# A decoder block with 32 experts on one core: expert weights in 4-MB loads, and four blocks of the next expert ahead of a down product

## The chip, the cores and the metric

The kernel runs on one core of one Trainium2 chip. The metric is device time in microseconds. Three runs of the kernel before took 1317.76, 1319.06 and 1319.45 us; the median is 1319.06.

## The reference

One decoder block over 256 tokens of 1024 features in float32: a hybrid mixer (state space and gated branch), cross-attention into 256 memory tokens, and a layer of 32 experts of which each token uses four. Most of the weights, 32 x 12 MB, belong to the experts:

```python
logits = (xt @ w_router + b_router)
top_v, top_i = lax.top_k(logits, 4)
gates = sum(one_hot(top_i, 32) * softmax(top_v)[..., None], axis=1)
def expert_step(acc, p):
    wgu, bgu, wd, bd, g = p
    hgu = xt @ wgu + bgu                       # 1024 -> 2 x 1024
    gate = minimum(hgu[:, :1024], 7.0)
    up = clip(hgu[:, 1024:], -7.0, 7.0)
    y = ((up + 1.0) * gate * sigmoid(1.702 * gate)) @ wd + bd
    return acc + g[:, None] * y
x = LN(ALPHA * x + acc)
```

## The kernel before, in words

The first stage, until about 392 us, does mixer, attention and router. Its weights come in 1-MB units, which are split in two parts for exact float32 products. It then turns to the experts, and nearly all that the change touches is there.

The experts run one after the other, each with room for 64 tokens (`CAP`); two neighbours make a `Pair`. Per pair, `onehot` builds a selection matrix, four `gather` calls (four products of PE each) collect the tokens' features of the pair, one eviction by ACT and one by DVE behind each, and `weights` prepares the scatter. Per expert, `gate_up` returns two functions. `products(k)` multiplies block k of 128 input features: four products of 512 columns, two each for gate and up, which run side by side in two column halves of PE. There are eight blocks an expert. `swiglu` adds the bias by four bf16 products, and runs the chain gc, sg, uc, gc, uc: minimum on DVE, sigmoid on ACT, clip, product and last product on DVE. `hidden_t` transposes the result uc by four PE transpositions and copies it to hT on ACT. `down` multiplies hT with the 4 MB of down weights, 16 products into y. After the second expert of a pair `scatter` copies y to ys (three ACT copies) and adds the pair's outputs to the tokens by four products and four DVE additions into acc, which lies in the tile cd.

`expert_w` loads the weights. The order of use is one long stream of units of 1 MB, a slot of 8192 bytes a partition. The first 22 units are loaded into slots that the first stage frees (`FIRST`); all later ones go round a ring of 20 slots in units of two, 2 MB, one DMA on SyncE's (SP's) queue with rows of 16384 bytes. A unit is issued when the products that read the slots before are done, and each SP issue waits behind the one before it. The last ten loads are 1 MB again. In the source, two blocks (`AHEAD = 2`) of the next expert stand between an expert's swiglu and its hidden_t. The engines run their instructions in the order of the built program; the framework orders them when it builds it, from the source's order, the dependencies and a cost model of its own, so the source's order is not always the program's.

Three pieces of work stand between the experts: `overflow_table` after expert 14, `add_rest` after expert 16 (the residual and the bias of the down product, with 32-row products; its bias rows come by two SP loads into tiles that scatter uses too), and `last_norm` after expert 20. The last expert's down product is cut in four pieces of 256 columns (`down_piece`, `scatter_piece`), then `finish` normalizes and stores.

Of the kernel before, what the change touches and what calls it, by code (L numbers as in the profile page):

```python
# [49 lines left out]
def block_kernel(ctx: ExitStack, tc: tile.TileContext, a, out):  # L50
# [13 lines left out]
    big = ctx.enter_context(tc.tile_pool(name="big", bufs=1))  # L64

    def two(tag, dt=F32):

        return big.tile([P, 2, 2048], dt, tag=tag, name=uniq(tag))
# [134 lines left out]
    def w_parts():  # L203
        t = two(("t01", "t23")[tcount[0] % 2], F32R).rearrange("p q (i c) -> p q i c", i=2)
        tcount[0] += 1
        return [[t[:, q, i] for q in range(2)] for i in range(2)]
# [123 lines left out]
    mh, ml = feat("ab")  # L330
# [32 lines left out]
    xh, xl = feat("xhl")  # L363
# [21 lines left out]
    gvu = two("ab")  # L385
    gv = gvu[:, 0].rearrange("p (c d) -> p c d", c=2)
# [20 lines left out]
    uT = gvu[:, 1].rearrange("p (k t) -> p k t", k=KB)  # L407
# [192 lines left out]
    ysh, ysl = feat("ab")  # L600
# [81 lines left out]
    mh, ml = feat("ab")  # L682
# [13 lines left out]
    xh, xl = feat("xhl")  # L696
# [294 lines left out]
    ucount = [0]  # L991

    def expert_w(src, apart=False):

        i = ucount[0]
        ucount[0] += 1
        if 2 * i < len(FIRST):
            t = []
            for h in range(2):
                name = FIRST[2 * i + h]  # L1000
                with tc.issue_after(wload[PHASE_A.index(FIRST_AFTER.get(name, ("wo", 3)))].ins):
                    if name in SLOTS:
                        t.append(bt(name))
                    elif name == "d":
                        t.append(cd[:, 1])
                    else:
                        if h == 0:
                            both = two(name)
                        t.append(both[:, h])
                    nc.sync.dma_start(t[h], src[:, h])  # L1010
            return t
        name = RING[(i - len(FIRST) // 2) % len(RING)]
        if name in SLOTS:
            at = SLOTS.index(name)
            t = arena[:, at:at + 2, :]
        else:
            t = two(name)
        if apart:
            for h in range(2):
                nc.sync.dma_start(t[:, h], src[:, h])  # L1020
        else:
            nc.sync.dma_start(t, src)
        return [t[:, h] for h in range(2)]

    def gate_up(src, sel, xe, before=None, last=False):
# [40 lines left out]
    def down(src, odd, hT, y, apart=False, between=None):  # L1066

        for u in range(2):
            if u and between is not None:
                between()  # L1070
            w = expert_w(src(u), apart)
            for b in range(4):
                k = 4 * u + b
                for n in range(2):
                    o = 64 * (n ^ odd)
                    te.matmul(y[n][o:o + 64, :], hT[:, b, 64 * u:64 * u + 64],  # L1076
                              w[b // 2][:, b % 2 * D + n * 512:b % 2 * D + (n + 1) * 512], start=(k == 0), stop=(k == KB - 1))

    def scatter(y, PT, first=False):
        ys = [wk.tile([P, 512], F32, tag="ux", name=uniq("ys")) for n in range(2)]  # L1080
        se.activation(ys[0], y[0], AF.Copy)  # L1081
        se.activation(ys[1][0:64, :], y[1][64:128, :], AF.Copy)
        se.activation(ys[1][64:128, :], y[1][0:64, :], AF.Copy)
        for n in range(2):
            for c in range(2):
                ps = pst("sm", 2)
                te.matmul(ps, PT[:, c, :], ys[n], start=True, stop=True)  # L1087
                av = acc[:, c, n * 512:(n + 1) * 512]
                if first:
                    ve.tensor_copy(av, ps)  # L1090
                else:
                    ve.tensor_tensor(av, ps, av, ALU.add)  # L1092
# [42 lines left out]
    AHEAD = 2  # L1135
# [20 lines left out]

    def begin(e):
        xg = pairs[e // 2].xg
        current[e] = gate_up(lambda u: a["w_gu"][e, u], i96[:, e:e + 1], lambda k: xg[:, k, e % 2 * CAP:(e % 2 + 1) * CAP],
                             lambda k: before(e, k), e == NE - 1)  # L1160
# [4 lines left out]
    for e in range(NE - 2):  # L1165
# [3 lines left out]
        uc = swiglu()  # L1169
# [19 lines left out]
    for k in range(AHEAD, KB):  # L1189
        current[ea][0](k)  # L1190
    uc = current[ea][1]()
    begin(eb)
    for k in range(AHEAD):
        current[eb][0](k)
    hT = hidden_t(uc)
    for k in range(AHEAD, KB):
        current[eb][0](k)
# [3 lines left out]
    down(lambda u: a["w_down"][ea, u], 0, hT, y, True, lambda: hTb.append(hidden_t(uc)))  # L1201
# [3 lines left out]
    PT = pairs[ea // 2].PT  # L1205
    for q in range(4):
        if q % 2 == 0:
            w = expert_w(a["w_last"][q // 2], True)
        down_piece(hTb[0], w[q % 2], q, ys)
        if q:  # L1210
            scatter_piece(ys, PT, q - 1, st)
# [5 lines left out]
    with tc.For_i(0, nx, 1):  # L1217
# [36 lines left out]
        down(lambda u: a["w_down"][bass.ds(ev, 1), u].rearrange("e p h d -> p (e h) d"), 0, hT, y)  # L1254
# [12 lines left out]
        for i in range(2):  # L1267
# [9 lines left out]
FIRST = ["e1", "k", "g", "gb", "xhl", "xhl", "w3", "w4", "e0", "x0", "ab", "ab", "w5", "w0", "w1", "w2", "t01", "t01", "t23",  # L1277
         "t23", "j", "d"]
SLOTS = ["e1", "k", "g", "gb", "w3", "w4", "e0", "x0", "w5", "w0", "w1", "w2", "j", "h"]
FIRST_AFTER = {"e1": ("z", 1), "k": ("wq", 0), "g": ("wq", 1), "gb": ("wo", 0)}  # L1280

RING = FIRST[0:20:2]

# [15 lines left out]
def arrange(inputs):  # L1299
# [31 lines left out]
    r["w_gu"] = wg.reshape(NE, 4, 2, P, 2 * D).transpose(0, 1, 3, 2, 4)  # L1331
    r["w_down"] = wd.reshape(NE, 2, 4, P, D).transpose(0, 1, 3, 2, 4).reshape(NE, 2, P, 2, 2 * D)
    r["w_last"] = wd[NE - 1].reshape(KB, P, 4, 256).transpose(2, 1, 0, 3).reshape(2, 2, P, 2 * D).transpose(0, 2, 1, 3)
# [22 lines left out]
```

## Time and profile before

| | |
|---|---|
| median of the runs | 1319.06 us |
| the profiled execution's own time | 1316.82 us |
| its span | 1315.1 us |
| PE busy | 1250.8 us, 95% |
| DVE busy | 450.3 us, 34% |
| ACT busy | 315.5 us, 24% |
| bytes by DMA | 472.00 MB, mean 359 GB/s |

The span is the time from the first to the last instruction. A busy time is the sum of the stretches in which an engine has an instruction at work; PE's products are pipelined, and a product in float32 appears as two records. The chain that ended last is 75% PE and 18% DMA over the whole span. A wait is told with what ended it.

### The profile page before, as it was taken

The page shows a single profiled execution, that of the slowest core. Times are in us where ns is not written, and L with a number is a line of the kernel's source. Part 1 is how long each engine was busy: PE and PEld are TensorE (multiplying, and loading weights), DVE is VectorE, ACT ScalarE, POOL GpSimd, SP SyncE. Part 2 cuts the span into 40 slices and gives each one's busy share as a digit, 9 for nine tenths or more (in the row PEclk, how much of TensorE's full clock was granted, in tenths as well). Part 3 has the DMA queues.
Part 4 walks back from the last instruction along what each step waited for, and adds up shares of the span by engine and source line. Part 5 has one row for each costly group of instructions (what it writes and reads, how often), then busy time and mean ns, then how long its engine had stood idle before and what let it go on. Part 6 is the DMA issues. An engine that isn't in the chain of part 4 may idle for free.

```text
span 1315.1 us, 15885 instructions
## 1 busy us (share of the span) xinstructions
PE 1250.8 (95%) x6757; PEld 684.9 (52%) x6758; DVE 450.3 (34%) x791; ACT 315.5 (24%) x536; POOL 29.1 (2%) x49
## 2 busy tenths in 40 slices
PE   6999999999999999999999999999999999989895
PEld 6899899989873443343333433333343433323232
DVE  4569766687441212121221112232221212212124
ACT  4746665444531111111111111101110111101000
POOL 2110000001000000000000000000000000000000
PEclk9999999999999999999999999969999999999998
DMA  9655543586788999999999999999999999999993
GB/s 357 239 176 196 192 161 133 184 290 227 275 322 353 425 426 427 427 427 428 429 428 427 428 428 427 412 428 427 427 428 428 427 428 427 428 427 427 428 424 160
DMA packets 43930, 472.00 MB, mean 359 GB/s; under 512 B 5104, under 2 KB 6928, under 8 KB 10064
## 3 DMA queue, kind: packets, MB, share of 16 engines
q1 hardware_dynamic: 39840, 464.41, 85.9%
q10 hardware_dynamic: 4016, 6.55, 1.6%
q8 instruction: 54, 0.88, 0.3%
q14 instruction: 20, 0.16, 0.0%
HBM read 469.49 MB, written 1.05 MB: 358 GB/s over the span
## 4 chain that ended last, share of the span: by engine, by line
PE 75%; DMA 18%; DVE 3%; ACT 2%; issue 1%; POOL 1%; ACTq 0%; DVEq 0%; SPq 0%; POOLq 0%
PE gu L1037 25%; PE y L1076 14%; DMA t<-in_w_gu_dram 6%; PE mm L255 6%; PE mm L239 5%; PE mm L238 5%; PE mm L237 5%; PE sm L971 4%; PE sm L1087 3%; DMA arena<-in_w_down_dram 3%; DMA ab<-in_w_gu_dram 3%; DMA arena<-in_w_gu_dram 3%; DMA t<-in_w_down_dram 2%; PE sm L1062 1%; DVE t L181 1%
## 5 line engine op out<-in xcount | busy, mean ns | idle before, releaser
L1037 PE MATMUL gu<-arena,cd 128*64 128x512 f32 x1240 | 279.8, 594 | 4.8 <-DMA arena<-in_w_gu_dram 4.8
L1037 PEld LDWEIGHTS gu<-arena,cd 128*64 128x64 f32 x1240 | 86.6, 137 | 171.5 <-issue 157.1
L181 DVE TENSOR_TENSOR t<-arena,t 128x1024 fp32r<-128x1024 f32 (+1 forms) x111 | 131.9, 1210 | 49.6 <-ACT t L180 49.6
L1076 PE MATMUL y<-arena,hT 128*64 128x512 f32 x592 | 140.7, 616 | 6.8 <-ACT hT L1063 5.6
L180 ACT ACTIVATE t<-arena 128x1024 fp32r<-128x1024 f32 (+1 forms) x114 | 113.8, 1038 | 59.2 <-PE mm L255 19.1
L1049 DVE TENSOR_SCALAR gc<-gu 128x512 f32<-128x512 f32 x32 | 22.1, 692 | 297.9 <-PE gu L1044 297.9
L237 PE MATMUL mm<-xhl,t 128*128 128x256 f32 x384 | 110.5, 288 | 0.0
L239 PE MATMUL mm<-xhl,t 128*128 128x256 f32 x384 | 108.8, 283 | 1.7 <-DVE t L181 1.7
L238 PE MATMUL mm<-xhl,t 128*128 128x256 f32 x384 | 108.7, 283 | 0.0
L1050 ACT ACTIVATE sg<-gc 128x512 f32<-128x512 f32 x32 | 20.2, 630 | 342.1 <-DVE gc L1049 342.1
L975 DVE TENSOR_SCALAR cd<-sm,par 128x128 f32<-128x128 f32 x64 | 26.2, 410 | 210.7 <-ACT cd L973 210.5
L1092 DVE TENSOR_TENSOR cd<-sm,cd 128x512 f32<-128x512 f32 x56 | 38.7, 692 | 169.3 <-PE sm L1087 169.3
L1076 PEld LDWEIGHTS y<-arena,hT 128*64 128x64 f32 x592 | 42.6, 140 | 85.9 <-issue 74.7
L1037 PE MATMUL gu<-t,cd 128*64 128x512 f32 x384 | 87.1, 595 | 0.1
L973 ACT ACTIVATE cd<-sm,par 128x128 f32<-128x128 f32 x64 | 29.3, 457 | 227.4 <-PE sm L971 226.0
L971 PEld LDWEIGHTS sm<-pair,arena 128*128 128x128 f32 x512 | 62.0, 191 | 31.7 <-issue 27.2
L239 PEld LDWEIGHTS mm<-xhl,t 128*128 128x128 f32 x384 | 73.5, 191 | 1.9 <-DVE t L181 1.9
L971 PE MATMUL sm<-pair,arena 128*128 128x128 f32 x512 | 71.3, 285 | 3.2 <-ACT pair L989 1.8
L238 PEld LDWEIGHTS mm<-xhl,t 128*128 128x128 f32 x384 | 73.6, 192 | 0.2
L237 PEld LDWEIGHTS mm<-xhl,t 128*128 128x128 f32 x384 | 73.5, 191 | 0.2
L1087 PE MATMUL sm<-ys,pair 128*128 128x512 f32 x120 | 59.1, 615 | 10.4 <-ACT ys L1081 10.2
L1037 PEld LDWEIGHTS gu<-t,cd 128*64 128x64 f32 x384 | 26.5, 137 | 50.3 <-issue 48.3
(314 smaller groups left out, 1447.8 us busy)
## 6 DMA issues: line engine op xcount, KB each, us to landing
arena<-in_w_gu_dram SPq DMA_DIRECT2D x71, 2048.0 KB, 31.8
arena<-in_w_down_dram SPq DMA_DIRECT2D x35, 2048.0 KB, 30.0
arena<-in_wa_dram SPq DMA_DIRECT2D x56, 1024.0 KB, 5.1
t<-in_w_gu_dram SPq DMA_DIRECT2D x22, 2048.0 KB, 33.8
ab<-in_w_gu_dram SPq DMA_DIRECT2D x13, 2048.0 KB, 30.1
xhl<-in_w_gu_dram SPq DMA_DIRECT2D x12, 2048.0 KB, 29.5
t<-in_w_down_dram SPq DMA_DIRECT2D x12, 2048.0 KB, 30.9
arena<-in_w_gu_dram SPq DMA_DIRECT2D x13, 1024.0 KB, 7.3
```

The source lines that it names most:

```text
L180: se.activation(h, src, AF.Copy)
L181: sub_op[0] = (eng or ve).tensor_tensor(l, src, h.bitcast(F32), ALU.subtract)
L237: te.matmul(ps[:, b, :], wh, xh[:, k, :], start=(k == 0), stop=False)
L238: te.matmul(ps[:, b, :], wh, xl[:, k, :], start=False, stop=False)
L239: te.matmul(ps[:, b, :], wl, xh[:, k, :], start=False, stop=(k == KB - 1))
L255: last[0] = te.matmul(res[c], x[:, k, c * P:(c + 1) * P], w[k // 2 % 2][:, k % 2, :], start=(k == 0 and i == 0), stop=(k == KB - 1 and i = ...
L971: te.matmul(pg[:, b, :], x2[:, c, k * P:(k + 1) * P], self.t[:, 0, c, :], start=(c == 0), stop=(c == 1))
L973: se.activation(self.xg[:, k, :], pg[:, 0, :], AF.Identity, bias=b2[:, k:k + 1], scale=g2[:, k:k + 1])
L1037: te.matmul(t[64 * j:64 * j + 64, :], xe(k), ws[k][:, n * D + j * 512:n * D + (j + 1) * 512], start=(k == 0), stop=False)
L1076: te.matmul(y[n][o:o + 64, :], hT[:, b, 64 * u:64 * u + 64], w[b // 2][:, b % 2 * D + n * 512:b % 2 * D + (n + 1) * 512], start=(k == 0), ...
L1087: te.matmul(ps, PT[:, c, :], ys[n], start=True, stop=True)
L1092: ve.tensor_tensor(av, ps, av, ALU.add)
```

## The change

The slots of the ring that were pairs of tiles (`t01`, `t23`, `xhl`, `ab`) become two tiles of four slots, `four0` and `four1`; the other slots lie in fours in the arena. From expert 4 on, a ring load is 4 MB, four slots with rows of 32768 bytes, half of an expert's gate and up weights or all its down weights; experts 0 to 3 keep 2 MB, the last expert and the last down products take smaller ones. The packing of the weights in HBM follows. `AHEAD` is 4, with hidden_t after the third block; scatter is returned as a function that is called behind block 4 of the next expert, whose first four blocks come before the down product; its two half copies change places. The bias rows of the down product go by one load into the free slot `j`, and two tiles of the first stage move to the slots `h` and `j`.

```diff
+    def fours(i, dt):
+        if (i, dt) not in four:
+            four[i, dt] = big.tile([P, 4, 2048], dt, tag=f"four{i}", name=uniq(f"four{i}"))
+        return four[i, dt]
...
-        bd = [wk.tile([NE, 512], F32, tag="ux", name=uniq("bd")) for n in range(2)]
-        for n in range(2):
-            nc.sync.dma_start(bd[n], a["b_down"][:, n * 512:(n + 1) * 512])
+        t = bt("j")
+        nc.sync.dma_start(t[:NE, :D], a["b_down"])
+        bd = [t[:NE, n * 512:(n + 1) * 512] for n in range(2)]
...
+    def expert_w(src, n=1):
+        out = []
+        h = src.shape[1]
+        while len(out) < h:
+            i = ucount[0]
+            if i < len(FIRST):
+                m, name = 1, FIRST[i]
...
+            else:
+                m = min(n, h - len(out))
+                at = (rcount[0] + NRING - len(FIRST) % 4) % NRING
+                assert at % m == 0
+                rcount[0] += m
+                t = slots(RING[at // 4] + at % 4, m)
+                after = ExitStack()
+            ucount[0] += m
+            with after:
+                nc.sync.dma_start(t, src[:, len(out):len(out) + m])
+            out += [t[:, q] for q in range(m)]
+        return out
...
-            if k % 2 == 0:
-                ws[k], ws[k + 1] = expert_w(src(k // 2), last and k == KB - 2)
+            if k % 4 == 0:
+                ws.update(enumerate(expert_w(src(k // 4), n_rows[k // 4]), k))
...
-    AHEAD = 2
+    AHEAD = 4
...
+    def rows_of(e):
+        return (2, 2) if e < 4 else (4, 4)
...
+    ready = []
+    def finish_products(e):
         products, swiglu = current.pop(e)
         for k in range(AHEAD, KB):
             products(k)
+            if ready:
+                ready.pop()()
+        return swiglu()
+
+    for e in range(NE - 2):
+        uc = finish_products(e)
         begin(e + 1)
-        for k in range(AHEAD):
+        for k in range(AHEAD - 1):
             current[e + 1][0](k)
         hT = hidden_t(uc)
+        current[e + 1][0](AHEAD - 1)
...
-        down(lambda u: a["w_down"][e, u], b, hT, y)
+        down(a["w_down"][e], b, hT, y, rows_of(e)[0])
         if b:
...
-            scatter(y, pairs.pop(e // 2).PT, e == 1)
+            ready.append(scatter(y, pairs.pop(e // 2).PT, e == 1))
...
-    down(lambda u: a["w_down"][ea, u], 0, hT, y, True, lambda: hTb.append(hidden_t(uc)))
+    down(a["w_down"][ea], 0, hT, y, 2, lambda: hTb.append(hidden_t(uc)))
...
-FIRST = ["e1", "k", "g", "gb", "xhl", "xhl", "w3", "w4", "e0", "x0", "ab", "ab", "w5", "w0", "w1", "w2", "t01", "t01", "t23",
-         "t23", "j", "d"]
...
+FIRST = ["e1", "k", "g", "gb", "w5", "w0", "xh", "xl", "a", "b", "e0", "x0", "w1", "w2", "j", "w3", "w4", "t0", "t1", "t2", "t3", "d"]
+RING = [8, 0, 12, 4, 16]
...
-    r["w_gu"] = wg.reshape(NE, 4, 2, P, 2 * D).transpose(0, 1, 3, 2, 4)
+    r["w_gu"] = wg.reshape(NE, 2, 4, P, 2 * D).transpose(0, 1, 3, 2, 4)
```

The built program moves instructions in more places than the diff. In the rows below a name before the arrow is what is written; gu_51 and gu_52 are gate and up of expert 25, uc_26 is expert 25's result of swiglu, hT_26 its transposed copy; i96 and bgs stand for the bias products.

PE from the last bias product of expert 25, the second of its pair, to its transpositions; first before, then after the change:

```order
L1044 LDWEIGHTS i96_109
L1044 MATMUL gu_52_6537<-bgs_873,i96_109 64x512
L1037 MATMUL gu_53_6651<-arena_61,cd_4_3791 64x512 x2
L1037 MATMUL gu_54_6652<-arena_61,cd_4_3791 64x512 x2
L1037 MATMUL gu_53_6651<-arena_61,cd_4_3791 64x512 x2
L1037 MATMUL gu_54_6652<-arena_61,cd_4_3791 64x512 x2
L1062 MATMUL sm_226_6663<-ident_86,uc_26_6645 128x128 x4
L1076 MATMUL y0_13_6561<-arena_61,hT_26_6662 64x512
```

```order
L1055 LDWEIGHTS i96_109
L1055 MATMUL gu_52_6356<-bgs_860,i96_109 64x512
L1073 MATMUL sm_226_6480<-ident_86,uc_26_6458 128x128 x4
L1048 MATMUL gu_53_6464<-four0_2_3788,cd_4_3731 64x512 x2
L1048 MATMUL gu_54_6465<-four0_2_3788,cd_4_3731 64x512 x2
L1048 MATMUL gu_53_6464<-four0_2_3788,cd_4_3731 64x512 x2
```

The transpositions move from behind two blocks of the next expert to straight behind the bias products; four blocks now stand between them and the down product.

PE at the same place of expert 24, the first of its pair, where gathers of the next pair (sm from pair_14) stand near; first before, then after:

```order
L1044 MATMUL gu_50_6440<-bgs_873,i96_109 64x512
L1037 MATMUL gu_51_6536<-arena_61,cd_4_3791 64x512 x2
L1037 MATMUL gu_52_6537<-arena_61,cd_4_3791 64x512 x2
L1037 MATMUL gu_51_6536<-arena_61,cd_4_3791 64x512 x2
L1037 MATMUL gu_52_6537<-arena_61,cd_4_3791 64x512 x2
L1062 MATMUL sm_221_6555<-ident_86,uc_25_6530 128x128 x4
L971 MATMUL sm_222_6583<-pair_14_6508,arena_61 128x128 x4
```

```order
L1055 MATMUL gu_50_6264<-bgs_860,i96_109 64x512
L980 MATMUL sm_220_6357<-pair_14_6328,arena_61 128x128 x4
L980 MATMUL sm_221_6373<-pair_14_6328,arena_61 128x128 x4
L1073 MATMUL sm_222_6385<-ident_86,uc_25_6349 128x128 x4
L980 MATMUL sm_223_6414<-pair_14_6328,arena_61 128x128 x4
L997 MATMUL sm_224_6429<-ident_86,G_13_6426 128x128 x2
L1048 MATMUL gu_51_6355<-four1_2_3895,cd_4_3731 64x512 x2
```

Here two gathers stand between bias and transpositions in place of two blocks of products.

PE in the tail, the four pieces of the last down product (y0, y1) and the scatter pieces (sm from ys); first before, then after:

```order
L1099 MATMUL y0_17_7272<-t23_47_7269,hT_32_7247 64x256 x8
L1108 MATMUL sm_256_7294<-ys_31_7265,pair_16_6932 128x256
L1099 MATMUL y1_17_7283<-t23_47_7269,hT_32_7247 64x256 x8
L1108 MATMUL sm_257_7298<-ys_31_7265,pair_16_6932 128x256
L1108 MATMUL sm_258_7315<-ys_31_7265,pair_16_6932 128x256
L1099 MATMUL y0_18_7304<-arena_61,hT_32_7247 64x256 x8
```

```order
L1113 MATMUL y0_17_7053<-arena_61,hT_32_7030 64x256 x8
L1113 MATMUL y1_17_7064<-arena_61,hT_32_7030 64x256 x8
L1122 MATMUL sm_256_7075<-ys_31_7045,pair_16_6730 128x256
L1122 MATMUL sm_257_7079<-ys_31_7045,pair_16_6730 128x256
L1113 MATMUL y0_18_7083<-arena_61,hT_32_7030 64x256 x8
L1122 MATMUL sm_258_7094<-ys_31_7045,pair_16_6730 128x256
```

The second piece moves ahead of the first piece's scatter.

## Rows read from the trace of the kernel before

**Rows 1.** Windows: stretch and length, busy us (count) by engine, PEclk, DMA share, GB/s.

```profile
420.00:830.00 410.00, 398.71 (x1899) 152.97 (x1897) 79.39 (x164) 47.30 (x89) 0.00 (x0) 1.00 1.01 427
900.00:1240.00 340.00, 324.10 (x1548) 124.25 (x1546) 63.32 (x120) 40.79 (x76) 0.00 (x0) 1.00 1.01 428
...
1272.00:1288.00 16.00, 14.44 (x68) 4.49 (x64) 2.97 (x5) 1.48 (x3) 0.00 (x0) 1.00 1.01 421
```

**Rows 2.** PE's timeline, scatters (start, us, line, tiles, [idle before]).

```profile
450.12 3.96 PE L1087 MATMUL sm<-ys,pair 128*128 128x512 f32 x8 [0.59 <-ACT ys L1081]
...
773.55 3.95 PE L1087 MATMUL sm<-ys,pair 128*128 128x512 f32 x8 [0.68 <-ACT ys L1081]
...
831.70 3.96 PE L1087 MATMUL sm<-ys,pair 128*128 128x512 f32 x8 [0.68 <-ACT ys L1081]
...
907.63 3.96 PE L1087 MATMUL sm<-ys,pair 128*128 128x512 f32 x8 [0.73 <-ACT ys L1081]
...
1245.78 3.96 PE L1087 MATMUL sm<-ys,pair 128*128 128x512 f32 x8 [0.68 <-ACT ys L1081]
```

**Rows 3.** Waits of PE, 420 to 830 (total us, times, longest).

```profile
PE y L1076 <- ACT hT L1063: 4.8, 7, 0.7
PE sm L1087 <- ACT ys L1081: 4.7, 7, 0.7
```

**Rows 4.** Waits of PE, 900 to 1290.

```profile
PE gu L1037 <- DMA arena<-in_w_gu_dram: 4.8, 6, 1.2
...
PE gu L1037 <- DMA ab<-in_w_gu_dram: 2.8, 3, 1.3
```

**Rows 5.** Timeline of all engines, 1276 to 1283, expert 31's swiglu.

```profile
1277.75 0.60 PE L1044 MATMUL gu<-bgs,i 96*64 96x512 bf16 x4
...
1278.18 0.69 DVE L1049 TENSOR_SCALAR gc<-gu 128x512 f32<-128x512 f32 x1 [14.53 <-PE gu L1044]
...
1278.97 0.63 ACT L1050 ACTIVATE sg<-gc 128x512 f32<-128x512 f32 x1 [12.73 <-DVE gc L1049]
...
1279.63 0.69 DVE L1052 TENSOR_TENSOR gc<-gc,sg 128x512 f32<-128x512 f32 x1 [0.16 <-ACT sg L1050]
1280.36 0.69 DVE L1053 SCALAR_TENSOR_TENSOR uc<-uc,gc 128x512 f32<-128x512 f32 x1
...
1281.19 0.63 PE L1062 MATMUL sm<-ident,uc 128*128 128x128 f32 x4 [0.88 <-DVE uc L1053]
```

**Rows 6.** PE's timeline: two gathers; four blocks of an expert.

```profile
631.80 2.07 PE L971 MATMUL sm<-pair,arena 128*128 128x128 f32 x16
...
750.17 7.04 PE L1037 MATMUL gu<-t,cd 128*64 128x512 f32 x32
```

**Rows 7.** Groups by line, DVE, 420 to 830 (busy us, mean ns, idle).

```profile
L975 DVE TENSOR_SCALAR cd<-sm,par 128x128 f32<-128x128 f32 x30 | 12.3, 410 | 101.4 <-ACT cd L973 101.3
```

**Rows 8.** Windows: the stretch at half the clock.

```profile
857.40:877.90 20.50, 20.50 (x47) 7.34 (x48) 6.77 (x11) 0.00 (x0) 0.00 (x0) 0.50 1.01 429
```

**Rows 9.** PE's timeline around expert 17's down product.

```profile
851.45 0.66 PE L1062 MATMUL sm<-ident,uc 128*128 128x128 f32 x4
...
852.85 2.05 PE L937 MATMUL sm<-gr,ident 32*128 32x128 f32 x16 [0.53 <-ACT hT L1063]
855.42 1.09 PE L930 MATMUL sm<-bd,gT 32*128 32x512 f32 x2 [0.53 <-PE sm L937]
...
872.87 6.98 PE L1076 MATMUL y<-arena,hT 128*64 128x512 f32 x18
```

**Rows 10.** PE's timeline in the tail.

```profile
1288.49 1.95 PE L1099 MATMUL y<-t,hT 128*64 128x256 f32 x16 [0.81 <-DVE ys L1203]
1291.36 0.70 PE L1108 MATMUL sm<-ys,pair 128*128 128x256 f32 x2 [0.93 <-DVE ys L1103]
...
1301.90 1.16 PE L1108 MATMUL sm<-ys,pair 128*128 128x256 f32 x4 [0.31 <-DVE ys L1103]
```

**Rows 11.** The chain that ended last (start, us, what).

```profile
1261.00 24.69 DMA t<-in_w_down_dram
```

More of the change, by code (lines that the diff above doesn't have):

```diff
@@ L384, in block_kernel @@
     gbm = bt("g").rearrange("p (g d) -> p g d", g=2)
[L385 to L386 removed]
+    gv = bt("h").rearrange("p (c d) -> p c d", c=2)
     st = stats_tile(2)
@@ L991, in block_kernel @@
     ucount = [0]
[L993 to L1023, printed above, removed]
@@ L1025, in gate_up, with slots @@
-    def gate_up(src, sel, xe, before=None, last=False):
+    rcount = [0]
+    def slots(i, n):
+        if i < len(SLOTS_R):
+            return fours(i // 4, F32)[:, i % 4:i % 4 + n, :]
+        i -= len(SLOTS_R)
+        return arena[:, i:i + n, :]
+    def expert_w(src, n=1):
[5 more added lines that the diff above has]
+                m, name = 1, FIRST[i]
+                if name == "d":
+                    t = cd[:, 1:2]
+                else:
+                    t = slots((SLOTS_R + SLOTS).index(name), 1)
+                after = tc.issue_after(wload[PHASE_A.index(FIRST_AFTER.get(name, ("wo", 3)))].ins)
+            else:
+                m = min(n, h - len(out))
[9 more added lines that the diff above has]
+        return out
@@ L1027, in gate_up @@
+    def gate_up(src, sel, xe, before=None, n_rows=(4, 4)):
         gp, up = pst("gu", 4), pst("gu", 4)
@@ L1064, in hidden_t, with down, scatter, go @@
         return hT
-    def down(src, odd, hT, y, apart=False, between=None):
-        for u in range(2):
-            if u and between is not None:
+    def down(src, odd, hT, y, rows=4, between=None):
+        w = expert_w(src, rows)
+        for k in range(KB):
+            if k == 4 and between is not None:
                 between()
[L1071 to L1079, printed above, removed]
+            for n in range(2):
+                o = 64 * (n ^ odd)
+                te.matmul(y[n][o:o + 64, :], hT[:, k % 4, 64 * (k // 4):64 * (k // 4) + 64],
+                          w[k // 2][:, k % 2 * D + n * 512:k % 2 * D + (n + 1) * 512], start=(k == 0), stop=(k == KB - 1))
+    def scatter(y, PT, first):
         ys = [wk.tile([P, 512], F32, tag="ux", name=uniq("ys")) for n in range(2)]
         se.activation(ys[0], y[0], AF.Copy)
+        se.activation(ys[1][64:128, :], y[1][0:64, :], AF.Copy)
         se.activation(ys[1][0:64, :], y[1][64:128, :], AF.Copy)
[L1083 to L1092, printed above, removed]
+        def go():
+            for n in range(2):
+                for c in range(2):
+                    ps = pst("sm", 2)
+                    te.matmul(ps, PT[:, c, :], ys[n], start=True, stop=True)
+                    av = acc[:, c, n * 512:(n + 1) * 512]
+                    if first:
+                        ve.tensor_copy(av, ps)
+                    else:
+                        ve.tensor_tensor(av, ps, av, ALU.add)
+        return go
     def down_piece(hT, w, q, ys):
@@ L1159, in begin @@
         current[e] = gate_up(lambda u: a["w_gu"][e, u], i96[:, e:e + 1], lambda k: xg[:, k, e % 2 * CAP:(e % 2 + 1) * CAP],
-                             lambda k: before(e, k), e == NE - 1)
+                             lambda k: before(e, k), (4, 2) if e == NE - 1 else rows_of(e))
     begin(0)
@@ L1186, in block_kernel @@
                 acc = cd[:, 1].rearrange("p (c d) -> p c d", c=2)
-            scatter(y, pairs.pop(e // 2).PT, e == 1)
+            ready.append(scatter(y, pairs.pop(e // 2).PT, e == 1))
     ea, eb = NE - 2, NE - 1
-    for k in range(AHEAD, KB):
-        current[ea][0](k)
-    uc = current[ea][1]()
+    uc = finish_products(ea)
     begin(eb)
-    for k in range(AHEAD):
+    for k in range(AHEAD - 1):
         current[eb][0](k)
     hT = hidden_t(uc)
-    for k in range(AHEAD, KB):
+    for k in range(AHEAD - 1, KB):
         current[eb][0](k)
```

38 lines of the change are left out of this document (20 added, 18 removed).

## The prediction

> **What bounds the kernel now.** I read the profile from the outside in: the windows by stage, the waits of the tensor engine (PE), its timeline around one pair of experts, and the tail. In the expert stage two resources are nearly full. The DMA engines move 427 to 428 GB/s at a share of 1.01 without a break [rows 1]. A pair of experts is 24 loads of 1,048,576 bytes, 25.17 MB, so the stream needs 25.17 / 0.428 = 58.8 us for it. PE is busy 97% of 420 to 830 and waits there for the two ACT copies, not for loads [rows 1, 3]. From one scatter of a pair to the next it takes, from 450.12 to 773.55, six periods of 53.9 us [rows 2]. PE is thus the faster one by 4.9 us a pair, but it starts behind, with 22 loads already in the ring. Only after 900 does it wait for loads, never longer than 1.3 us [rows 4]. At the last scatter, at 1245.78, it has caught up. Let it run at its own pace from 450.12: 14 periods give 1204.7. Two pairs were longer than 53.9: 831.70 to 907.63 took 75.9 (the rest of the sum, and the slow clock), 773.55 to 831.70 took 58.2 (the overflow table) [rows 2]; that adds 22.0 and 4.2, 1230.9 in all. The gap to 1245.78, 14.9 us, is all the slack that PE has against the stream. This is the number to remember: PE work of more than 14.9 us that is added before the last scatter comes out at the end, whatever the loads do.
>
> **The change part by part.** *Loads of 4 MB in rows of 32768 bytes.* The 1-MB loads of the end, in rows of 8192 bytes, ran at 421 GB/s, the 2-MB ones in rows of 16384 at 428 [rows 1]. That doubling gave 1.6%; half as much for the next, 0.8% of the stream between 430 and 1240, is 6 us. Below, the row may cost as much a byte as now, or 6 us more if long rows stall. I take 4 us less for the stream, and nothing for the sum, as long as PE is what ends last. The Trainium skill (DMA: Bandwidth & Descriptors, section Measured) lists 341 GB/s for 1 MB and 425 for 16 MB, so larger transfers should gain a good deal; the trace has 428 at 2 MB already, and by that table the gain is used up. A four is freed and landed as a whole; PE, some 30 us behind the stream, has the next ones in the ring, so this costs nothing until it catches up.
>
> *The order on PE.* Here is the cost. In the source four blocks of the next expert stand around the transpositions of hidden_t. In the built program they stand behind them: from expert 4 on, the transpositions come straight after the bias products in experts 4, 5, 7, 9 to 29 and 30 (15 places), and behind two gathers in experts 6, 8 to 28 (12 places); the first and second order pairs of the section on the change show both. Transposing needs uc, the end of the swiglu chain. The chain is seen bare in the tail: bias ends at 1278.35, then gc, sg, gc and uc on DVE and ACT, and the transposition starts at 1281.19: 2.84 us [rows 5]. Before, two blocks of products (3.5 us) covered it. Behind two gathers the cover is 2.07 us [rows 6], and the first eviction of a gather, 0.41 us, stands in DVE's queue ahead of the last swiglu operation [rows 7]: 2.84 + 0.41 - 2.07 = 1.18 us uncovered. Queued behind the waiting transposition on PE are all products of the next expert; nothing on PE passes it.
>
> Up to the last scatter: 14 x 2.84 = 39.8, 12 x 1.18 = 14.2. Gone is the wait of the down product for hT, since four blocks now lie between: 7 in six and a half pairs at 0.69 [rows 3], one a pair, 13 x 0.69 = 9.0. Net 45.0 us, three times the slack. The chain can't be shorter than its four operations, 2.6 us, and may be 0.5 longer with a busier DVE: 40 to 55. The two long pairs keep their 26.2; the 32-row products of the rest of the sum stand in another mix, with blocks of products between, and the bias rows no longer wait in SP's queue, so 10 less or 5 more there. Last scatter: 1230.9 + 45.0 = 1275.9.
>
> *Scatter behind a block.* From expert 3 on it stands straight behind the down product as before, with its wait of 0.68 [rows 2]; only the first pair's is behind a block. Nothing. The swapped copies on ACT: nothing, the first copy is what PE waits for. Packing and slots of the first stage: loads of t0 to t3 are issued together after the last wo product, at most 5 us later, and are used 30 us after: nothing.
>
> *The tail.* From the last scatter PE runs by itself: four scatter products 3.9, four blocks 7.0 [rows 6], bias 0.6, the wait 2.84, transpositions 0.6, eight blocks of expert 31 14.0, bias 0.6, the down product 3.5 + 0.6 + 3.5 (its second hidden_t is covered by the first half): 37.1. Then 0.8 to the first piece of the last down product. The pieces took from 1288.49 to 1303.06 with 1.86 of waits (0.93 and three of 0.31) [rows 10]; now two pieces stand ahead of the first scatter piece (third order pair), so only the last 0.31 stays: 13.0. From there to the end of the span 12.0 as before. 1275.9 + 37.1 + 0.8 + 13.0 + 12.0 = 1338.8.
>
> *The clock.* It fell once in this stage: the stretch 857.40 to 877.90 has a granted clock of 0.50, 1.2 GHz for 2.4 [rows 8]. Before it PE had done 6 us of transpositions and 32-row products with 1.06 us of idle; it rose after products had run for 5.0 us from 872.87 [rows 9]. Each new place is 4.0 us with 2.84 idle, and only bias products and transpositions around. A fall there, with full products behind it, costs at most half of 5.0, 2.5 us; at no fall nothing. 15 places: 0 to 37. Nothing in the trace has just this mix; by idle time it is poorer than the stretch that fell, by length shorter. I take 1.0 a place, 15 us. The Trainium skill (TensorE: Matmul & The Clock Gate, section Why this matters for your kernels) warns against long idle gaps between bursts of matmuls, because they put the clock back to half rate. [...]
>
> Span 1338.8 + 15 = 1354. The profiled execution took 1316.82 for a span of 1315.1, 1.7 more, and the median of the runs is 2.2 above that: 1358. The forecast is slower by 3%.
>
> **The rivals.** *The stream stays the bound (faster).* The new waits fall where PE would wait for a load anyway. Then the end is the stream's: the last load on which the tail waited, 24.69 us from 1261.00 [rows 11], lands at 1285.69 less 4; a 2-MB half has to be multiplied after it instead of 1 MB, 1.7 more; the pieces save 1.6. 1316.8 - 4 + 1.7 - 1.6 = 1313, 1315 as a median. For it: the DMA share of 1.01, and the 7.6 us that gate and up products wait for loads after 900 [rows 4]. Against: PE has only 14.9 us of slack. It decides if the net new waits stay under that, that is if a bare place costs under 1.7 us instead of 2.84 (14 x 1.7 - 9.0; the places behind gathers then cost nothing).
>
> *No fall of the clock.* All else as forecast: 1338.8 + 1.7 + 2.2 = 1343. For it: the tail's waits of 0.93 between pieces did not bring it down while they lasted [rows 10]; against it, those places are a third as long.
>
> *A fall at every place.* 1338.8 + 37 + 3.9 = 1380. Then a pair takes 53.9 + 3.3 for the waits + 2.8 for the clock (15 places in 13.5 pairs), 60 us, slower than the stream's 58.8, and DMA would show gaps.
>
> *The change doesn't do what it says*, as far as the order goes: that is built into the sum, since the order shows it.
>
> **How the numbers follow.** Chances: a part of the places fall (forecast, 1358) 45%; no fall 25%; all fall 20%; the stream bound 7%; something that makes PE equal to before, 3%. The range leaves out the stream-bound case and the ends: from no fall with 10 us less in the rest of the sum, 1333, less a shorter chain, 1328; up to all places falling, 1380. What runs of this kernel can tell is about 0.2%, 2.6 us: slower takes the three cases above 1322 (90%), faster 6%, the same 4%.
>
> **What would show it.** In the new profile the waits of PE must have a line "transposition (sm) waiting for DVE uc" with about 27 waits, none over 3.5 us, 50 to 60 us in sum; the hT waits go to nearly none; scatters come 57 us or more apart and the last of a whole pair starts near 1276 to 1300; windows of the expert stage show a granted clock under 1.00 in several places; loads of 4 MB land at 427 GB/s or more while the queue is full, but the mean rate of the stage falls below 428. The forecast is wrong if PE's waits for uc sum to under 20 us, or if PE waits for loads by more than 20 us in the stage: then the stream still sets the time.

## The result: 1358.2 us, 3.05% slower

The changed kernel takes 1358.19 us (median of 4 runs, 1357.97 to 1359.32); the kernel before took 1319.15 beside it. The ratio is 1.0305, with a 95% interval of 1.0292 to 1.0317. The forecast was 1358 and slower. The profiled execution has a span of 1356.6 us.

### The profile after

The windows of the kernel after (columns as in [rows 1]):

```profile
420.00:830.00 410.00, 381.65 (x1795) 146.82 (x1793) 75.53 (x160) 45.97 (x87) 0.00 (x0) 0.98 1.00 427
900.00:1240.00 340.00, 313.04 (x1440) 119.95 (x1438) 57.77 (x111) 38.28 (x72) 0.00 (x0) 0.96 0.96 405
...
1099.80:1106.50 6.70, 6.01 (x16) 2.19 (x18) 0.64 (x1) 0.60 (x1) 0.00 (x0) 0.50 1.03 445
```

Against [rows 1], PE's busy time in the first stretch falls from 398.71 to 381.65, and in the second the stream is no longer continuous: a share of 0.96 and 405 GB/s for 428. The stream now waits for PE to free slots. The third line is one of many short stretches at half the clock, where before there was one long one [rows 8].

What PE waits for after 420 (us in total, times, the longest):

```profile
PE sm L1073 <- DVE uc L1064: 53.1, 27, 2.8
PE sm L1099 <- ACT ys L1091: 9.7, 14, 0.7
PE sm L980 <- ACT pair L998: 1.7, 3, 0.6
...
PE y L1113 <- ACT ys L1229: 0.8, 1, 0.8
```

This is the new picture in four lines: 27 waits of the transposition for the end of the swiglu chain, where before there was none over 420 to 1290 but the one in the tail. The down product's waits for hT of [rows 3] and the load waits of [rows 4] have no line any more. PE never waits for a load; it is the bound by itself.

A place is where the transpositions of one expert stand on PE; a bare place has nothing between the bias products and them, a gathers' place has two gathers there. PE's timeline: scatters that answer to [rows 2], a gathers' place (693.85), and a bare place with what follows it (1097.15 to 1110.95):

```profile
693.85 0.63 PE L1073 MATMUL sm<-ident,uc 128*128 128x128 f32 x4 [0.99 <-DVE uc L1064]
...
1097.15 0.60 PE L1055 MATMUL gu<-bgs,i 96*64 96x512 bf16 x4
1100.49 1.11 PE L1073 MATMUL sm<-ident,uc 128*128 128x128 f32 x4 [2.74 <-DVE uc L1064]
1101.54 9.58 PE L1048 MATMUL gu<-arena,cd 128*64 128x512 f32 x32
1110.95 7.03 PE L1085 MATMUL y<-four,hT 128*64 128x512 f32 x32
1118.67 3.96 PE L1099 MATMUL sm<-ys,pair 128*128 128x512 f32 x8 [0.69 <-ACT ys L1091]
...
1293.50 3.96 PE L1099 MATMUL sm<-ys,pair 128*128 128x512 f32 x8 [0.69 <-ACT ys L1091]
```

Read 1097.15 downwards: the bias products end, PE stands for 2.74 us, then transposes at 1.11 us for 0.63, then does four blocks in 9.58 us that take 7.04 at full clock [rows 6]. The gap costs twice. The last whole pair's scatter has moved from 1245.78 to 1293.50, 47.7 us. From there to the end of the span it takes 63.1 us (1356.6 - 1293.50), where before it took 69.3.

Where the time went, in one list: 47.7 us before the last scatter, 6.2 given back behind it, 41.5 in the span.

### The profile page after: what moved, and what is told of

It reads as the page before. It is cut to its first block, busy times and chain, and to the rows that moved or that the text cites. A ratio compares the mean times of both kernels' runs of the same rounds, so it can differ in the third digit from the quotient of the medians.

```text
span 1356.6 us, 15797 instructions
## 1 busy us (share of the span) xinstructions
PE 1263.9 (93%) x6758; PEld 692.1 (51%) x6758; DVE 447.6 (33%) x791; ACT 322.0 (24%) x536; POOL 29.5 (2%) x49
## 4 chain that ended last, share of the span: by engine, by line
PE 90%; DVE 6%; ACT 2%; issue 1%; DMA 0%; ACTq 0%; DVEq 0%
PE gu L1048 35%; PE y L1085 16%; PE mm L265 8%; PE mm L248 5%; PE mm L249 5%; PE mm L247 5%; PE sm L1099 4%; PE sm L980 3%; PE sm L1073 2%; DVE gc L1060 1%; DVE gc L1063 1%; DVE uc L1064 1%; ACT sg L1061 1%; PE sm L946 1%; PE gu L1055 1%
## 5 line engine op out<-in xcount | busy, mean ns | idle before, releaser
L1048 PE MATMUL gu<-arena,cd 128*64 128x512 f32 x1240 | 290.1, 619 | 0.0
L1048 PE MATMUL gu<-four,cd 128*64 128x512 f32 x800 | 187.2, 621 | 0.0
L191 DVE TENSOR_TENSOR four<-arena,four 128x1024 fp32r<-128x1024 f32 (+1 forms) x119 | 137.8, 1168 | 83.4 <-ACT four L190 80.6
L190 ACT ACTIVATE four<-arena 128x1024 fp32r<-128x1024 f32 (+1 forms) x122 | 122.2, 1014 | 103.1 <-PE mm L248 49.0
L247 PE MATMUL mm<-four,four 128*128 128x256 f32 x496 | 142.1, 287 | 0.0
L248 PE MATMUL mm<-four,four 128*128 128x256 f32 x496 | 140.5, 283 | 0.0
L249 PE MATMUL mm<-four,four 128*128 128x256 f32 x496 | 140.5, 283 | 0.0
L1085 PE MATMUL y<-arena,hT 128*64 128x512 f32 x576 | 131.7, 605 | 0.0
L1048 PEld LDWEIGHTS gu<-four,cd 128*64 128x64 f32 x800 | 57.6, 142 | 115.4 <-issue 114.6
L247 PEld LDWEIGHTS mm<-four,four 128*128 128x128 f32 x496 | 95.1, 192 | 0.2
L248 PEld LDWEIGHTS mm<-four,four 128*128 128x128 f32 x496 | 95.1, 192 | 0.2
L249 PEld LDWEIGHTS mm<-four,four 128*128 128x128 f32 x496 | 95.0, 192 | 0.0
L1085 PE MATMUL y<-four,hT 128*64 128x512 f32 x416 | 91.9, 594 | 0.0
L1085 PEld LDWEIGHTS y<-arena,hT 128*64 128x64 f32 x576 | 41.5, 140 | 82.4 <-issue 81.5
L1073 PE MATMUL sm<-ident,uc 128*128 128x128 f32 x128 | 23.6, 309 | 53.1 <-DVE uc L1064 53.1
```

What stands on the lines that cost most here:

```text
L190: se.activation(h, src, AF.Copy)
L191: sub_op[0] = (eng or ve).tensor_tensor(l, src, h.bitcast(F32), ALU.subtract)
L247: te.matmul(ps[:, b, :], wh, xh[:, k, :], start=(k == 0), stop=False)
L248: te.matmul(ps[:, b, :], wh, xl[:, k, :], start=False, stop=False)
L249: te.matmul(ps[:, b, :], wl, xh[:, k, :], start=False, stop=(k == KB - 1))
L1073: te.transpose(pt[:, f, :], uc[:, f * P:(f + 1) * P], ident)
```

## The experiments

Theory A is the prediction's: PE is the bound, its new waits come from the order, the clock adds to them. Theory B: the 4-MB loads cost by themselves. Theory C: both, or the clock alone.

### Load size by order

*4-MB loads, transpositions late.* In the changed kernel, with `block[0]` the last product issued:

```diff
+        with tc.issue_after(block[0].ins):
             for f in range(4):
                 te.transpose(pt[:, f, :], uc[:, f * P:(f + 1) * P], ident)
```

> The changed kernel with one thing put back: the transpositions of hidden_t are held on the tensor engine until three blocks of the next expert have been issued; loads of 4 MB, ring, packing and tail stay. Theory A (the loss is the order on the tensor engine, with the clock that falls in its gaps): the wait of the transposition for the swiglu chain is covered by 5 us of products, PE runs at about 54 us a pair again, the stream sets the end, and its longer rows and the pieces of the tail come out: 1308 to 1317 us, no clock fall outside of the rest of the sum. Theory B (the 4-MB loads cost by themselves, since a four is freed and landed as a whole): PE waits for loads and the time stays above 1335. Theory C (half and half): near 1335.

Measured: **1307.44 us** (1307.16 to 1307.84), 0.9924 of before (0.9911 to 0.9937). One edit turns 3% slower into 0.8% faster. Its windows and its waits of PE after 420:

```profile
420.00:830.00 410.00, 396.92 (x1883) 151.53 (x1881) 78.08 (x164) 47.12 (x89) 0.00 (x0) 0.99 1.00 428
900.00:1240.00 340.00, 323.01 (x1542) 125.27 (x1540) 61.76 (x120) 40.39 (x76) 0.00 (x0) 0.99 1.00 431
```

```profile
PE sm L1101 <- ACT ys L1093: 9.5, 14, 0.7
PE sm L980 <- ACT pair L998: 6.7, 11, 0.6
PE y L1087 <- DMA four<-in_w_down_dram: 4.0, 2, 2.0
PE gu L1049 <- DMA arena<-in_w_gu_dram: 3.9, 2, 2.2
PE y L1087 <- DMA arena<-in_w_down_dram: 2.4, 2, 2.0
PE gu L1049 <- DMA four<-in_w_gu_dram: 2.4, 2, 2.2
```

No line for uc is left, load waits are back (12.7 us in four lines), and the stream runs at 431 GB/s. One pair of places in PE's timeline shows why:

```profile
701.92 0.60 PE L1056 MATMUL gu<-bgs,i 96*64 96x512 bf16 x4
702.36 5.32 PE L1049 MATMUL gu<-arena,cd 128*64 128x512 f32 x24
707.61 0.66 PE L1075 MATMUL sm<-ident,uc 128*128 128x128 f32 x4
```

The same chain runs, under 5.32 us of products, and PE has nothing to wait for. The expectation missed a detail: besides the rest of the sum the clock falls for short stretches at two more places, near 801 and 988 us.

*2-MB loads, the order left to the framework:*

```diff
-        return (2, 2) if e < 4 else (4, 4)
+        return (2, 2)
...
```

> The changed kernel with loads of 2 MB in rows of 16384 bytes throughout, nothing held by hand. In the built program the transpositions then stand behind two blocks of the next expert, as in the kernel before, so that the load size is what moved them. Theory A: 1314 to 1320 us, equal to before but for the pieces of the tail (less 1.6) and a 2-MB half at the end (plus 1.7); transpositions wait for the swiglu chain under 0.3 us a place. Theory B: also about 1317, and only the run with 4 MB in the late order tells the two apart. If it stays near 1358, something else of the change costs (packing, slots, bias rows): neither theory.

Measured: **1314.19 us**, ratio 0.9974 (0.9963 to 0.9985). The source's order is untouched, yet in the built program the transpositions stand behind two blocks:

```profile
646.85 0.60 PE L1055 MATMUL gu<-bgs,i 96*64 96x512 bf16 x4
647.28 3.60 PE L1048 MATMUL gu<-four,cd 128*64 128x512 f32 x16
650.82 0.66 PE L1073 MATMUL sm<-ident,uc 128*128 128x128 f32 x4
```

So the load size moved the instructions on PE. Packing, slots, the bias rows, the new tail and two more blocks ahead of the down product together give 0.26%.

*2-MB loads, the changed kernel's order by hand* (transpositions straight behind the bias products or two gathers, products held behind them):

```diff
...
+                    with tc.issue_after(held[0].ins) if held[0] is not None else ExitStack():
+                        te.matmul(t[64 * j:64 * j + 64, :], xe(k), ws[k][:, n * D + j * 512:n * D + (j + 1) * 512],
...
```

> The kernel with the new packing and tail, but loads of 2 MB in rows of 16384 bytes (as in the earlier run at 2 MB, which took 1314), and the changed kernel's order on the tensor engine put in by hand from expert 4 on: transpositions straight behind the bias products at the odd experts, behind two gathers at the even ones. It completes the table of load size (2 or 4 MB) by order (late or early). Theory A (the order is all of the loss): 1352 to 1362 us, pairs 58 to 58.9 us apart, about 53 us of waiting for the swiglu chain, no waits for loads. Theory B (4-MB loads are needed for the loss): 1314 to 1330.

Measured: **1354.33 us**, ratio 1.0284 (1.0268 to 1.0300). Its first line of waits of PE after 420:

```profile
PE sm L1078 <- DVE uc L1068: 51.4, 27, 2.8
```

The four kernels make the table:

| us | transpositions late | transpositions early |
|---|---|---|
| 2-MB loads | 1314.2 | 1354.3 |
| 4-MB loads | 1307.4 | 1358.2 (the change) |

The order costs 40 us at 2 MB and 51 at 4 MB. The late kernels also differ in that the transpositions stand behind two blocks at 2 MB and behind three at 4 MB, so the 6.8 us between them are those of the 4-MB loads and of that block together. In the early order the 4-MB kernel is 3.9 us worse; the pair of experts 4 and 5 is 3.1 us longer there (expert 4's place is bare in the changed kernel, while the hand-made order has gathers in it) and the pair with the rest of the sum 3.7. Theory B is out: without 4-MB loads nearly all of the loss is there, and with them, in the other order, none.

### What the clock costs

*The early order in the kernel before* (the next expert's products are held behind the transpositions, as above):

```diff
...
+        hT = hidden_t(uc)
         begin(e + 1)
         for k in range(AHEAD):
             current[e + 1][0](k)
-        hT = hidden_t(uc)
```

> The kernel before, 2-MB loads, two blocks ahead, all else as it was; only the transpositions of hidden_t now stand straight behind the bias products (or behind the first gathers) and the next expert's products behind them. Theory A: this alone gives the loss of the changed kernel: about 26 waits of 2.7 us for the swiglu chain, clock falls in about 12 places, scatters 57.5 to 58.5 us apart, 1345 to 1360 us. Two blocks between the transpositions and the down product instead of four leave the wait for hT covered. Theory B (4-MB loads cost): 1319 to 1325, since the stream hides the waits.

Measured: **1419.44 us**, ratio 1.0745 (1.0713 to 1.0777), far outside of what I expected. Its wait line and one place:

```profile
PE sm L1064 <- DVE uc L1055: 80.2, 30, 2.8
```

```profile
1214.98 0.60 PE L1046 MATMUL gu<-bgs,i 96*64 96x512 bf16 x4
1218.32 1.11 PE L1064 MATMUL sm<-ident,uc 128*128 128x128 f32 x4 [2.74 <-DVE uc L1055]
1219.37 4.63 PE L1039 MATMUL gu<-arena,cd 128*64 128x512 f32 x16
```

I had held the gathers' cover away: every place is bare, 30 waits of 2.7 us. So this is not the changed kernel's order, but the third rival's case, a fall of the clock at nearly every place: 27 of the 29 full waits have a stretch of 0.50 beginning within 4 us of the transposition's start. An undisturbed pair takes 60.6 to 63.9 us, some 62.6 in the mean; 53.9 - 0.7 (hT) + 2 x 2.71 is 58.6, so a place costs some 2 us on top of its wait. That is the clock's part in the main; 12 waits of 0.6 us for the scatter's matrix (pair) are in it too.

*Filling.* In the changed kernel, products whose result is thrown away, 11 at each place (`FILL`), between the bias products and the transpositions, and the next expert's products held behind these:

```diff
+        with tc.issue_after(bias[0].ins):
+            for _ in range(FILL):
+                last = te.matmul(pt.rearrange("p f js -> p (f js)"), onesB, onesB[:, 0:1].to_broadcast([P, 512]), start=True, stop=True)
```

> The changed kernel in its order, with 11 products of 512 columns whose results are thrown away (extra work, overwritten by the transpositions) between the bias products and the transpositions: PE is no longer idle while the swiglu chain runs, and its wait is not shortened. It measures the clock's term by itself. Theory A (clock part 1.7 us in each of 12 to 13 places): the clock stays at 1.00 outside of the rest of the sum, a pair takes 56.5 us, 1334 to 1342 us. If the falls don't depend on the idle gaps, or cost nothing: 1356 to 1362. If PE's order were not the bound: unchanged 1358.

Measured: **1372.34 us**, ratio 1.0417 (1.0402 to 1.0432): slower than the changed kernel, where I had expected 1334 to 1342. The clock did stay at 1.00 in the places, but the filling stood at the gathers' places too, where its 2.57 us came in place of a wait of 0.99, and most of the gathers moved behind the transpositions. A pair took 59.0. The edit was badly chosen and tells only that the stream is not the bound. The next run fills the bare places of the odd experts from 5 on, and leaves the others as they are:

```diff
...
+        bare = e > 4 and (e % 2 == 1 or e == NE - 2)
+        if bare:
+            hT = hidden_t(uc, FILL)
...
```

> The changed kernel with 11 extra products of 512 columns (thrown away, overwritten by the transpositions) only at the bare places, between the bias products and the transpositions of the odd experts from 5 on; the places behind two gathers are as in the changed kernel. In the earlier run with the filling everywhere it also stood at the gathers' places, where it took 2.6 us against 1.0 of waiting, and so hid what the clock gave back. Theory A (a fall of the clock costs some 1.3 us a pair): the clock stays at 1.00 outside of the rest of the sum, pairs come 56.6 to 57.2 us apart instead of 58.2, 1334 to 1341 us. If the clock costs nothing, or is not brought down by the gaps: 1355 to 1360.

Measured: **1335.31 us** (1333.41 to 1339.15), ratio 1.0138 (1.0119 to 1.0157), inside of what was expected. Its second window, its wait line, and a filled place:

```profile
900.00:1240.00 340.00, 327.63 (x1582) 129.12 (x1584) 62.11 (x121) 40.85 (x77) 0.00 (x0) 1.00 1.00 425
```

```profile
PE sm L1080 <- DVE uc L1066: 20.6, 27, 2.8
```

```profile
1196.22 2.57 PE L1077 MATMUL sm<-onesB 128*128 128x512 bf16 x11
1199.03 0.66 PE L1080 MATMUL sm<-ident,uc 128*128 128x128 f32 x4 [0.25 <-DVE uc L1066]
1199.61 7.09 PE L1050 MATMUL gu<-arena,cd 128*64 128x512 f32 x32
```

PE loses as much time at the place as in the changed kernel (2.57 + 0.25 against 2.74), but the clock is 1.00 and the four blocks take 7.09, not 9.58. Regular pairs are 56.6 us apart and not 58.2. So 22.9 us of the changed kernel's time are the clock's (1358.19 - 1335.31; 22.7 between the profiled spans): 1.5 to 2.0 in ten pairs, 2.9 and 5.1 in two with longer stretches at 0.50, less 1.7 in the pair of expert 4, whose place is not filled and has the longer stretch in the filled kernel. Work that is thrown away, in the place of idling, made the kernel that much faster.

### How much PE may lose before it shows

*Extra products in the kernel before*, 2, 5 and 9 an expert, ahead of the transpositions:

```diff
...
+        for _ in range(fill):
+            te.matmul(pt.rearrange("p f js -> p (f js)"), onesB, onesB[:, 0:1].to_broadcast([P, 512]), start=True, stop=True)
```

> The kernel before with 2 extra products of 512 columns (thrown away) for each of the experts 3 to 29, before the transposition that overwrites them: nothing on PE waits for them to be anything but PE work. One took 0.24 us at full clock in the earlier run with the filling. It weighs the slack of PE, which the prediction put at 14.9 us: 27 x 0.48 = 13.0 us of work, of which the wait of the down product for hT hides up to 6. If the slack is 14.9: no change beyond 1 us, 1317 to 1320, and waits for loads after 900 shorter than before's 7.6 us. If PE had no slack (theory C): 1324 to 1331.

> The same with 5 products an expert: 27 x 1.2 = 32.4 us of PE work, less the 9.0 of the waits for hT that it fills, less the slack of 14.9: 8.5 us come out at the end, 1322 to 1331. If the stream hid it all (slack above 25): 1317 to 1320.

> The same with 9 products an expert: 27 x 2.16 = 58.3 us, less 9.0 and 14.9: 34.4 us come out, 1346 to 1357, with no wait for loads left before the last scatter. From the runs with 5 and 9 the slack follows by a straight line: 25.9 us more of work, so 25.9 us more of time if both are past the slack.

Measured: **1345.65**, **1352.29** and **1371.79 us** (ratios 1.0201, 1.0271, 1.0412). All three are above what I expected, and the first by most. The waits of PE with 2 products an expert, after 420:

```profile
PE sm L971 <- DVE cd L975: 15.1, 19, 1.1
...
PE y L1078 <- ACT hT L1065: 9.7, 14, 0.7
PE sm L971 <- ACT hT L1065: 5.1, 10, 0.5
```

The extra products were put before the gathers, far ahead of the transpositions, and held one of the two buffers of sm. So the gathers waited for evictions, 20.2 us that the kernel before does not have, and the hT waits stayed. That is no measure of the slack; the load waits are gone in all three.

*Without a buffer:* two more sets of bias products with a selector of zeros (`more` is 2), experts 3 to 29.

```diff
...
+            for _ in range(more):
+                for n, t in ((0, gp), (1, up)):
+                    for j in range(2):
+                        c0 = n * D + j * 512
+                        te.matmul(t[64 * j:64 * j + 64, :], zsel.to_broadcast([96, CAP]), bg3[:, c0:c0 + 512],
+                                  start=False, stop=False)
...
```

> The filling of the last three runs held one of the two buffers of tile sm, and PE waited for it (15.1 us for DVE, 5.1 for ACT in the run with 2): they don't weigh the slack alone. Here the kernel before gets two more sets of bias products with a selector of zeros for each of the experts 3 to 29, in the same accumulation: no buffer, no new wait. Four take 0.43 us in the chain of waits, so 27 x 0.86 = 23.2 us of PE work. Before's own waits for loads are 7.9 us up to the last scatter and 2.4 behind it. If these are all of the slack (10.3): 12.9 us come out, 1327 to 1334. If the slack is the 14.9 of the prediction, with the same 2.4 behind it: 5.9 come out, 1321 to 1326.

Measured: **1329.03 us** (1328.24 to 1329.46), ratio 1.0084 (1.0070 to 1.0097): 11.3 us more. Its PE timeline, at the first pair's scatter, at one place with the added sets, behind the last norm's products, and at the last scatter; and a window:

```profile
450.98 3.96 PE L1093 MATMUL sm<-ys,pair 128*128 128x512 f32 x8 [0.58 <-ACT ys L1087]
...
659.01 1.03 PE L1045 MATMUL gu<-bgs,zsel 96*64 96x512 bf16 x8
659.88 0.60 PE L1050 MATMUL gu<-bgs,i 96*64 96x512 bf16 x4
...
1001.73 5.35 PE L1082 MATMUL y<-arena,hT 128*64 128x512 f32 x16
...
1261.54 3.96 PE L1093 MATMUL sm<-ys,pair 128*128 128x512 f32 x8 [0.68 <-ACT ys L1087]
```

```profile
1002.50:1005.50 3.00, 3.00 (x8) 0.73 (x6) 0.00 (x0) 0.00 (x0) 0.00 (x0) 0.50 1.01 431
```

The kernel before, around its last norm and at the scatter two pairs ahead of the last:

```profile
961.52 3.96 PE L1087 MATMUL sm<-ys,pair 128*128 128x512 f32 x8 [0.68 <-ACT ys L1081]
...
981.55 3.88 PE L937 MATMUL sm<-gr,ident 32*128 32x128 f32 x32
985.37 3.65 PE L1076 MATMUL y<-arena,hT 128*64 128x512 f32 x16
...
1020.12 3.96 PE L1087 MATMUL sm<-ys,pair 128*128 128x512 f32 x8 [0.68 <-ACT ys L1081]
...
1128.33 3.96 PE L1087 MATMUL sm<-ys,pair 128*128 128x512 f32 x8 [0.68 <-ACT ys L1081]
```

The set takes 0.87 us (659.01 to 659.88), 23.5 in 27 experts; 11.3 came out, 12.2 were hidden. No load wait is left in the trace, so PE runs at its own pace in it. Two things in its last scatter, at 1261.5, are not added work. This execution is 0.9 us late at the first pair's scatter already (450.98 for 450.12 [rows 2]), before the first added product. And it has a fall of the clock that the kernel before does not have: half a down product takes 5.35 us at 1001.73, where before it takes 3.65 at 985.37, so 1.7 us. PE's own pace for the kernel before is thus 1261.5 - 23.5 - 0.9 - 1.7 = 1235.5, and its slack 1245.8 - 1235.5 = 10.3. The trace of before says the same: its last two pairs, 1128.33 to 1245.78, in which nearly all load waits stand, take 117.5 us, 9.7 more than two periods of 53.9. The load waits up to the last scatter, added up over five lines, are 7.9: the idle time alone is less than what the waits cost. The prediction's 14.9 was 4.6 too high.

### Can more be had?

*The scatter really behind a block*, on top of the late order at 4 MB:

```diff
+                with tc.issue_after(block[0].ins):
                     ready.pop()()
```

> The 4-MB kernel in the late order (1307 us) with the scatter, besides, really held behind the first block of the next expert. PE no longer waits 0.69 us for the copies of y, 9.5 us in 14 places; but in that kernel the stream sets the pace of the last pairs, so theory A gives 1306 to 1307.5: at most the 0.7 us of the last place. If PE were still the bound, 1298 to 1300.

Measured: **1309.85 us**, ratio 0.9940 (0.9927 to 0.9954). The wait for ys, 9.5 us, is gone, and nothing was won; 1306 to 1307.5 had been expected. Its waits of PE, and one place and its window:

```profile
PE gu L1049 <- DMA arena<-in_w_gu_dram: 7.9, 6, 2.5
PE gu L1049 <- DMA four<-in_w_gu_dram: 7.7, 4, 2.5
...
PE y L1087 <- DMA arena<-in_w_down_dram: 5.2, 3, 2.0
PE y L1087 <- DMA four<-in_w_down_dram: 2.9, 2, 2.0
```

```profile
1239.43 8.78 PE L1087 MATMUL y<-arena,hT 128*64 128x512 f32 x32 [1.98 <-DMA arena<-in_w_down_dram]
```

```profile
1240.50:1243.80 3.30, 3.30 (x11) 1.11 (x9) 0.00 (x0) 0.00 (x0) 0.00 (x0) 0.50 1.04 447
```

Load waits went from 12.7 to 23.7 us: the 9.5 turned into waits for the stream. Behind the wait of 1.98 us shown the clock is at 0.50, and the down product takes 8.78 us for 7.04, close before the end. That would be 1.7 of the 2.4 us lost, but it is not shown: I did not test it apart, and the first run has five load waits as long (1.98 to 2.19 us) with no such fall.

*The same with 2-MB loads for the last three experts:*

```diff
-        return (2, 2) if e < 4 else (4, 4)
+        return (2, 2) if e < 4 or e > 28 else (4, 4)
```

> The same with the loads of the last three experts' gate and up products, and of expert 29's down product, in 2 MB instead of 4 MB, so that PE starts on them earlier and lags the stream less at the end (it started its last piece 2.2 us after the last load had landed). Theory A: 1304 to 1306.5. If long rows matter more in the last 100 us than the lag: 1307 to 1309.

Measured: **1307.07 us** (1306.69 to 1308.81), ratio 0.9922 (0.9908 to 0.9935), above the 1304 to 1306.5 of theory A. It takes back what the scatter's move lost and stands level with the first run. The best version is thus the changed kernel with its transpositions held behind three blocks: 1307.4, 0.8% faster than before.

## Why the prediction was right, step by step

**The bound, PE.** Right. PE has no load wait left, and the table shows that its order alone makes the loss.

**PE's own pace and the slack, 14.9 us.** Mis-sized: 10.3. I let PE run at 53.9 a pair and added two long pairs; a third was missed. The pair from 961.52 to 1020.12 takes 58.6 us without a load wait, as the 32 products of the last norm's rows (3.88 us at 981.55, expert 20) stand in it. That is 4.7 more than 53.9, and 1230.9 + 4.7 = 1235.6 is, within 0.1, the pace that the added work gave: this pair is the whole of the error. Being slower than thought, PE had less to lose: the error worked towards slower.

**The order, 45.0 us net.** The mechanism was right in each detail: 27 waits, 53.1 us in all where 27 waits in 50 to 60 were forecast; 2.74 at a bare place for 2.84, 0.99 behind gathers for 1.18, and no hT wait. But in the kernel without the clock's part (the bare places filled) pairs are 56.6 apart, 2.7 us more than before and not 45.0 / 13.5 = 3.3. That kernel's last scatter is at 1270.8, 35.3 behind PE's own pace of 1235.5 (and expert 4's place, not filled, still has its fall in there), so the term was some 10 us too large. The waits shown (2.74 and 0.99, less the 0.69 for hT) would make 3.04 a pair; why it is 2.7 stays open.

**The clock, 1.0 a place.** Too small, and for a wrong reason. I took it that some places would fall and others not. In the changed kernel 14 of the 15 bare places have a stretch at 0.50, and of the 12 places behind gathers none has but the one in the rest of the sum. The first window below is behind the one bare place without a stretch, expert 5's; the second is behind a bare place like the other 14.

```profile
547.80:551.20 3.40, 3.40 (x18) 1.46 (x20) 0.00 (x0) 0.60 (x1) 0.00 (x0) 1.00 0.83 357
...
720.92:724.32 3.40, 3.40 (x10) 1.37 (x12) 0.00 (x0) 0.60 (x1) 0.00 (x0) 0.50 1.00 426
```

By the filled kernel the falls cost 22.9 us, 1.6 in most pairs; the largest cost of a fall had been put at 2.5. That is the picture of the third rival (a fall at every place) at two thirds of its price, and that it comes to nearly the forecast's number is luck. A fall at every place had been given 20%. The Trainium skill (TensorE: Matmul & The Clock Gate, section Why this matters for your kernels) warns of long idle gaps between bursts of matmuls. The gaps that it names are longer than any here, so it does not say that these places fall: after gaps of 2.74 us the clock fell at 14 of 15, after gaps of 0.99 behind two gathers at none of 11. Nor was the one fall before a case of it: the idle times of PE ahead of it are 0.53 us each [rows 9].

**The sum.** Up to the last scatter: 1230.9 + 45.0 + 14.0 = 1289.9 forecast; 1235.5 + 35.3 + 22.7 = 1293.5 measured. Three terms were off by +4.6, -9.7 and +8.7, and mostly cancelled. So the number, right to 0.2 us, is luck; the direction, and the order as its main cause, are not.

**Loads of 4 MB.** The forecast gave them nothing as long as PE ends last: right. As a gain of the stream it took 4 us; in the late order they give at most 6.8, with the third block in it, near the upper estimate of 6. The Trainium skill (DMA: Bandwidth & Descriptors, section Measured) has 425 GB/s for 16 MB, measured on loads issued from GpSimd, and by the reading I gave it the gain was used up. These loads are issued from SP, and the late kernel's 431 beside 428 [rows 1] says that it was not.

**The scatter.** No effect, as forecast, since it was not moved; when it really is moved, in the late order, its 9.5 us turn into waits for loads.

**The tail.** 62.9 us from the last scatter to the end of the span without the clock (37.1 + 0.8 + 13.0 + 12.0); measured 63.1 with one fall in it, some 1.7 us by the other places. Right within 2 us.

## What to carry to other kernels

A change of load size can move instructions on an engine that it does not touch: read the built order, not the source, and hold what must not move by hand. Before pricing a new wait, find the slack pair by pair: ask of each that is longer than the others whether it waits for loads (9.7 us here in the last two, and 10.3 by added work) or has work of its own. A pace carried over pairs that are not all alike gave 14.9, the idle time of the load waits alone 7.9. A gap on PE has two prices, its length and the clock behind it; both were of weight here, 2.74 and 1.6 us.

## What was not expected of the hardware

- Loads of 4 MB in rows of 32768 bytes moved 431 GB/s over 900 to 1240, against 428 of 2 MB in rows of 16384, in the kernel before and in the 2-MB run alike. Load and row grew together, so which of the two does it is open.
- Throwing work into a gap paid: 11 useless products in each of 13 gaps of 2.74 us made the kernel 22.9 us faster.
- Gaps of 0.99 us behind two gathers left the clock alone. Waits of about 2 us for a load, with full products on either side, did both: of those of 1.9 us and more, four of seven in the late-scatter run came with a stretch at 0.50, none of five in the first run.
